# The last stage of an encoder layer: eight places for operand pieces, second halves loaded sooner, residual tiles in two sets

## The chip, the core and the metric

The kernel runs on one core of a Trainium2 chip. A core has a matrix engine (TensorE, PE in the rows), a vector engine (DVE), a scalar engine (ScalarE, ACT), GpSimd (POOL) and an engine that issues the transfers of this kernel (SyncE, SP; SPq is its queue). They run side by side, each takes its own instructions in a fixed order, and they wait for one another by semaphores. The metric is the time on the device in microseconds. TensorE's granted clock is given as a share of its full rate: 1.00 is the higher of its two levels, 2.4 GHz, and the lower one is 1.2 GHz.

## What is computed

One encoder layer on 9 blocks of 256 tokens (2048 of the prompt, 256 of the sample) with a model width of 1024. Cut to the part in which the change lies, with `o` the output of the gated linear attention (GLA), `y` that of the state-space branch (SSD) and `p` the embedding of each layer:

```python
def _layer(h, p, ...):
    u = _rmsnorm(h, norm_g)
    proj = u @ w_in                      # ... GLA gives o, SSD gives y
    o = _rmsnorm(o, gla_onorm_g).reshape(bt, L, GLA_VAL)
    o = o * jax.nn.silu(z_gla.astype(f32))
    y = y.reshape(bt, L, SSD_WIDTH) * jax.nn.silu(z_ssd.astype(f32))
    y = _rmsnorm(y, ssd_norm_g)
    mix = jnp.concatenate([o, y], axis=-1).astype(h.dtype)
    h = h + mix @ w_out
    e = _rmsnorm(p @ w_ple_proj, ple_norm_g)
    h = h + jax.nn.sigmoid(h @ w_ple_gate) * e
    return h
# trunk: _rmsnorm of the layer's output with final_norm_g
```

All is float32. Each product of two float32 matrices is made of three passes of rounded numbers: an operand is split into a rounded part (`_h`) and the rest (`_l`), and h·h, h·l and l·h are added up.

## The kernel before

Everything ahead of the last stage is the same in both kernels and isn't told here. The last stage, `output()` (L1232), works on blocks of 256 tokens and has three parts.

Part a, blocks 8 down to 0: `mix @ w_out` is split in two, and this is the GLA half. Four projections (`foa`, m = 0 to 3, 48 matmuls each) read the block's operand `fa{b}m`; the vector engine adds the residual tile `fx` (L1248) and SyncE stores the sum to `h1D`. The end of the stage before, the scan of the SSD branch (`s7b…`, `fz…zz`), still runs beside it and has its own few matmuls among the projections.

Part b, blocks 0 to 8: the SSD half, four projections `fob` from the operand `fb{b}m`, with the residual `fh` read back from `h1D` and the sum stored to `hD`.

Part c, the gate, blocks 0 to 8: class `Last` (L1135). Its `embed` makes `p @ w_ple_proj` (tiles `fl{b}e`), `load` (L1163) brings back the four tiles `fl{b}h` of h and splits each into a piece of the operand `fl{b}hh` (cast on the vector engine, L131, and the rest on GpSimd, L125), four projections `fpg` follow, `gate` (L1176) applies them (the product L1181 on the vector engine, the add L1182 and the sum of squares L1188 on GpSimd, squares on ScalarE), and `store` (L1226) multiplies the block with its norm (L1229) and writes the four tiles to `out` (L1230). In the loop (L1292 to L1310) the embedding of block b+1, the store of block b-1 and the load of block b+1 stand between the projections of block b.

An operand has four pieces, each with an h and an l tile of 128 x 2 x 256 (`new_u`, L151). They come from a pool with six places (`UBUFS`) for each of the two. A place comes free when the matmuls that read it are done, and a tile that is to take it waits for that. In parts a and b an operand (`mix_block`, L814) is made of two halves: each loads a raw tile (two places), scales it by the norm on the vector engine (L827; in part a by rows `fa{b}r` that SyncE loads, in part b by one made of `fb{b}r`), and splits it. The first half is issued with the operand, the second by `rest()`: in part a behind projection 2 of the block before (ahead of m = 3; for the last one ahead of m = 2), in part b ahead of m = 3.

Other tiles come from a second pool by tags: `dk` has 6 places and holds `fx` and `fh`, `mx` 7, `zo` 4, `eb` 2, `t4k` 2 and `y1` 10; `y1` holds the h tiles of the gate, four for each block. A scheduler walks through the program and fixes each engine's order; places that are handed out by the pools take part in it. So an edit of where a tile lies changes the order on all engines.

Of the kernel before, what the change touches and what calls it, by code (L numbers as in the profile page):

```python
# [9 lines left out]
F32R = mybir.dt.float32r  # L10
# [5 lines left out]
P = 128  # L16
T = 256
C = 128
NBP, NBS = 8, 1
NB = NBP + NBS  # L20
NT = NB * T
KT = 8
QMAX = 2
UK = 2
UBUFS = 6
# [8 lines left out]
def hybrid(ctx, tc, xT, pT, wsec, wsmall, wlast, wproj, wgate, bgate, norm_g, gla_g,  # L34
# [115 lines left out]

    def new_u(name):  # L151
        return [tuple(upool.tile([P, UK, T], F32R, name=f"{name}_{q}{n}", tag=f"u{q}", bufs=UBUFS)
                      for q in ("h", "l")) for n in range(KT // UK)]

    class Operand:

        def __init__(self, name, piece):
            self.parts, self.piece = new_u(name), piece
            for n in range(2):
                piece(n, *self.parts[n])  # L160
# [85 lines left out]
    with ExitStack() as mctx:  # L246
# [566 lines left out]

        def mix_block(b, half, r, name):  # L814

            raws = {}

            def piece(n, hi, lo):
                if n % 2 == 0:
                    r2 = upool.tile([P, 2, UK, T], F32, name=f"{name}_r{n}", tag="uraw", bufs=2)  # L820
                    sy.dma_start(r2, mixD[b][4 * half + n:4 * half + n + 2].rearrange("s p f t -> p s f t"))
                    raws[n], raws[n + 1] = r2[:, 0], r2[:, 1]
                raw = raws.pop(n)
                for k in range(UK):
                    kk = UK * n + k
                    g = g_gla[:, kk % 2:kk % 2 + 1] if half == 0 else g_ssd[:, kk:kk + 1]
                    ve.scalar_tensor_tensor(raw[:, k, :], raw[:, k, :], g, r(kk), ALU.mult, ALU.mult)  # L827
                split(raw, hi, lo, sc, po)
            return Operand(name, piece)

# [9 lines left out]
        def gla_mix(b, nm):  # L840
            r = [tmp("zo", [P, 2, T], f"{nm}r{j}") for j in range(2)]
            for j in range(2):
                rows(r[j], rD[b][2 * j:2 * j + 2])
            return mix_block(b, 0, lambda k: r[k // 4][:, k // 2 % 2, :], nm + "m")

# [23 lines left out]
        for i, s in enumerate(secs):  # L869
# [3 lines left out]
            for n, b in enumerate(s.order):  # L873
# [81 lines left out]
                u = u2  # L955
# [153 lines left out]
        def ssd_mix(b, nm):  # L1109
# [7 lines left out]
            def norm():  # L1117
                ps = bank("p2", [P, T], nm + "ps")
                total(ps, s, "hl", nm + "hl", ve, ve)
                rstd(ps, r, 1024.0, eps4)  # L1120
                return lambda: mix_block(b, 1, lambda k: r, nm + "m")

# [12 lines left out]
        class Last:  # L1135
# [27 lines left out]
            def load(self):  # L1163

                self.h = [tmp("y1", [P, 2, T], f"{self.nm}h{n}") for n in range(4)]
                self.uh = new_u(self.nm + "hh")
                for n in range(4):
# [64 lines left out]
        def output(nm, wo, u, first):  # L1232
# [3 lines left out]
            for b in range(NB - 1, -1, -1):  # L1236
                u2 = gla_mix(b - 1, f"{nm}a{b - 1}") if b else first_ssd()
                for m in range(4):
                    if m == (3 if b else 2):
                        u2.rest()  # L1240
                    x = tmp("dk", [P, 2, T], f"{nm}x{b}_{m}")
                    sy.dma_start(x, xT[b][:, 2 * m:2 * m + 2, :])
# [14 lines left out]
                if first:  # L1257
# [3 lines left out]
                    carry.append(lambda a=(s, bb, gate_z(z, f"{nm}z{bb}")): second(*a))  # L1261
            wp = [[tmp("xr" if q == 0 else "t4k", [P, 2, 512], f"{nm}wp{q}{j}", F32R) for j in range(2)] for q in range(2)]
            for b in range(NB):
# [4 lines left out]
                for m in range(4):  # L1268
                    if m == 3 and b + 1 < NB:
                        u2.rest()  # L1270
                    h = tmp("dk", [P, 2, T], f"{nm}h{b}_{m}")
                    sy.dma_start(h, h1D[b][:, 2 * m:2 * m + 2, :])
# [7 lines left out]
                    if b == NB - 1:  # L1280
# [3 lines left out]
                        wg.append(load_w(wlast[8 + m], f"{nm}g{m}"))  # L1284
                if b == NB // 2:
                    for j in range(2):
# [114 lines left out]
```

## Time and profile before

| | us |
|---|---|
| three runs | 2570.76, 2571.09, 2573.41 |
| median | 2571.09 |
| the profiled execution | 2570.19 |
| its span in the trace | 2568.5 |
| mean granted clock | 0.977 |

The profiled execution is 0.9 us below the median, and 1.7 us of it lie outside its span. In that span TensorE is busy for 2435.1 us (95%), the vector engine for 67%, ScalarE for 48% and GpSimd for 25%. The last stage runs from about 1749 us to the end: part a to 2007, part b to 2232, the gate from there on. In a row a duration of several like instructions in sequence is their sum ("x4"), and what stands in brackets at its end is how long the engine stood idle before it, and which instruction ended that. A granted clock below 1.00 means slower matmuls in a part of the stretch, and their cost comes on top of the idle time.

### The profile page before, as it was taken

The page shows a single profiled execution, that of the slowest core. Times are in us where ns is not written, and L with a number is a line of the kernel's source. Part 1 is how long each engine was busy: PE and PEld are TensorE (multiplying, and loading weights), DVE is VectorE, ACT ScalarE, POOL GpSimd, SP SyncE. Part 2 cuts the span into 40 slices and gives each one's busy share as a digit, 9 for nine tenths or more (in the row PEclk, how much of TensorE's full clock was granted, in tenths as well). Part 3 has the DMA queues.
Part 4 walks back from the last instruction along what each step waited for, and adds up shares of the span by engine and source line. Part 5 has one row for each costly group of instructions (what it writes and reads, how often), then busy time and mean ns, then how long its engine had stood idle before and what let it go on. Part 6 is the DMA issues. An engine that isn't in the chain of part 4 may idle for free.

```text
span 2568.5 us, 51535 instructions
## 1 busy us (share of the span) xinstructions
PE 2435.1 (95%) x19736; PEld 2373.7 (92%) x19736; DVE 1723.3 (67%) x4012; ACT 1225.5 (48%) x2468; POOL 638.5 (25%) x649
## 2 busy tenths in 40 slices
PE   7999999899999989999989999998999999998887
PEld 7999999799999979999989999998899999998886
DVE  8886799864579984468997456899633434544444
ACT  5565456644445654445565344565312323355545
POOL 3231000143200023320002330002444433354452
PEclk9999999899999999999999999999999999999988
DMA  6456466444655644465564446555765765412121
GB/s 235 161 175 196 154 181 206 154 139 146 217 169 166 194 143 161 146 205 170 168 215 138 137 154 214 168 164 176 230 196 186 239 184 159 133 38 75 38 75 60
DMA packets 295593, 415.05 MB, mean 162 GB/s; under 512 B 33020, under 2 KB 140328, under 8 KB 295336
## 3 DMA queue, kind: packets, MB, share of 16 engines
q1 hardware_dynamic: 295336, 411.66, 51.0%
q8 instruction: 157, 2.57, 0.4%
q14 instruction: 100, 0.82, 0.1%
HBM read 319.21 MB, written 92.35 MB: 160 GB/s over the span
## 4 chain that ended last, share of the span: by engine, by line
PE 58%; DVE 15%; DMA 10%; ACT 6%; issue 6%; POOL 4%; SPq 1%; DVEq 0%; POOLq 0%; ACTq 0%
PE pz L184 3%; PE pz L185 3%; PE pz L183 3%; PE pxb L183 2%; PE pxb L185 2%; PE pxb L184 2%; PE pxa L183 2%; PE fob L184 2%; PE pxa L184 2%; PE pxa L185 2%; PE fob L185 2%; PE fob L183 2%; PE pv L183 2%; PE pv L185 2%; PE pq L183 2%
## 5 line engine op out<-in xcount | busy, mean ns | idle before, releaser
L183 PE MATMUL pz<-u_h,wh_n 128*128 128x256 f32 x896 | 255.6, 285 | 0.0
L185 PE MATMUL pz<-u_h,wl_n 128*128 128x256 f32 x896 | 255.6, 285 | 0.0
L184 PE MATMUL pz<-u_l,wh_n 128*128 128x256 f32 x896 | 255.2, 285 | 0.0
L185 PEld LDWEIGHTS pz<-u_h,wl_n 128*128 128x128 f32 x896 | 171.0, 191 | 0.8 <-issue 0.7
L184 PEld LDWEIGHTS pz<-u_l,wh_n 128*128 128x128 f32 x896 | 171.0, 191 | 0.7 <-issue 0.7
L183 PEld LDWEIGHTS pz<-u_h,wh_n 128*128 128x128 f32 x896 | 171.0, 191 | 0.2
L183 PE MATMUL pxb<-u_h,wh_n 128*128 128x256 f32 x512 | 147.5, 288 | 0.0
L184 PE MATMUL pxa<-u_l,wh_n 128*128 128x256 f32 x512 | 147.2, 288 | 0.0
L183 PE MATMUL pxa<-u_h,wh_n 128*128 128x256 f32 x512 | 146.9, 287 | 0.0
L184 PE MATMUL pxb<-u_l,wh_n 128*128 128x256 f32 x512 | 146.3, 286 | 0.0
L185 PE MATMUL pxb<-u_h,wl_n 128*128 128x256 f32 x512 | 145.8, 285 | 0.0
L185 PE MATMUL pxa<-u_h,wl_n 128*128 128x256 f32 x512 | 145.4, 284 | 0.0
L183 PE MATMUL pq<-u_h,wh_n 128*128 128x256 f32 x384 | 113.3, 295 | 0.8 <-DVE z_0zz L805 0.5
L183 PE MATMUL pv<-wh_n,u_h 128*128 128x256 f32 x384 | 110.9, 289 | 0.7 <-DVE s4b1dm L508 0.2
L185 PE MATMUL pv<-wh_n,u_l 128*128 128x256 f32 x384 | 111.5, 290 | 0.0
L185 PE MATMUL pq<-u_h,wl_n 128*128 128x256 f32 x384 | 111.4, 290 | 0.0
L184 PE MATMUL pq<-u_l,wh_n 128*128 128x256 f32 x384 | 111.3, 290 | 0.0
L184 PE MATMUL pv<-wl_n,u_h 128*128 128x256 f32 x384 | 108.7, 283 | 0.0
L183 PEld LDWEIGHTS pxa<-u_h,wh_n 128*128 128x128 f32 x512 | 98.0, 191 | 1.6 <-issue 1.4
L183 PEld LDWEIGHTS pxb<-u_h,wh_n 128*128 128x128 f32 x512 | 97.9, 191 | 0.7 <-issue 0.7
L184 PEld LDWEIGHTS pxa<-u_l,wh_n 128*128 128x128 f32 x512 | 98.0, 191 | 0.5 <-issue 0.2
L184 PEld LDWEIGHTS pxb<-u_l,wh_n 128*128 128x128 f32 x512 | 97.8, 191 | 0.5 <-issue 0.5
(5981 smaller groups left out, 9539.6 us busy)
## 6 DMA issues: line engine op xcount, KB each, us to landing
u_h<-uD SPq DMA_DIRECT2D x224, 256.0 KB
u_l<-uD SPq DMA_DIRECT2D x224, 256.0 KB
wr_n<-wsec SPq DMA_DIRECT2D x48, 512.0 KB
fx<-xT SPq DMA_DIRECT2D x36, 256.0 KB
h1D<-fx SPq DMA_DIRECT2D x36, 256.0 KB
fh<-h1D SPq DMA_DIRECT2D x36, 256.0 KB
hD<-fh SPq DMA_DIRECT2D x36, 256.0 KB
wr_oa<-wlast SPq DMA_DIRECT2D x8, 512.0 KB
```

What stands on the lines that cost most here:

```text
L183: te.matmul(outs, lhsT=lh, rhs=rh, start=start and k == ks[0], stop=False, skip_group_check=True)
L184: te.matmul(outs, lhsT=lh, rhs=rl, start=False, stop=False, skip_group_check=True)
L185: te.matmul(outs, lhsT=ll, rhs=rh, start=False, stop=stop and k == ks[-1], skip_group_check=True)
```

## The change

Operands get eight places for pieces, by placing the second half of every other operand somewhere else. The second half of the GLA operands of even blocks below 7 and of the SSD operands of odd blocks below 7 lies in `t4k` (one tile for the h and the l of a piece); that of SSD block 7 and of the gate's even blocks lies in `eb` (piece 2) and `y1` (piece 3: two of the ten places). `rest()` is called ahead of m = 1 in part a and of m = 2 in part b. The residual tiles of odd m lie in `mx` (in part a for blocks below 7, in part b for all). The tiles of `wproj`, which use `t4k` too, are made and loaded behind block 6 of part b, no longer ahead of it and behind block 4.

```diff
-    def new_u(name):
-        return [tuple(upool.tile([P, UK, T], F32R, name=f"{name}_{q}{n}", tag=f"u{q}", bufs=UBUFS)
-                      for q in ("h", "l")) for n in range(KT // UK)]
+    def new_u(name, tags=()):
+        parts = []
+        for n in range(KT // UK):
+            tag = tags[n - 2] if tags and n >= 2 else None
+            if tag == "t4k":
+                t = tmp(tag, [P, 2, UK, T], f"{name}_{n}", F32R)
+                parts.append((t[:, 0], t[:, 1]))
+            elif tag:
+                parts.append(tuple(tmp(tag, [P, UK, T], f"{name}_{q}{n}", F32R) for q in "hl"))
+            else:
+                parts.append(tuple(upool.tile([P, UK, T], F32R, name=f"{name}_{q}{n}", tag=f"u{q}", bufs=UBUFS)
+                                   for q in ("h", "l")))
+        return parts
...
+            tags = ("t4k", "t4k") if b < NB - 2 and b % 2 == 0 else ()
+            return mix_block(b, 0, lambda k: r[k // 4][:, k // 2 % 2, :], nm + "m", tags)
...
+                tags = () if b % 2 == 0 else ("t4k", "t4k") if b < NB - 2 else ("eb", "y1")
+                return lambda: mix_block(b, 1, lambda k: r, nm + "m", tags)
...
-                self.uh = new_u(self.nm + "hh")
+                self.uh = new_u(self.nm + "hh", () if self.b % 2 else ("eb", "y1"))
...
-                    if m == (3 if b else 2):
+                    if m == (1 if b else 2):
                         u2.rest()
-                    x = tmp("dk", [P, 2, T], f"{nm}x{b}_{m}")
+                    x = tmp("mx" if m % 2 and b < NB - 2 else "dk", [P, 2, T], f"{nm}x{b}_{m}")
...
-            wp = [[tmp("xr" if q == 0 else "t4k", [P, 2, 512], f"{nm}wp{q}{j}", F32R) for j in range(2)] for q in range(2)]
...
-                    if m == 3 and b + 1 < NB:
+                    if m == 2 and b + 1 < NB:
                         u2.rest()
-                    h = tmp("dk", [P, 2, T], f"{nm}h{b}_{m}")
+                    h = tmp("mx" if m % 2 else "dk", [P, 2, T], f"{nm}h{b}_{m}")
...
-                if b == NB // 2:
+                if b == NB - 3:
+                    wp = [[tmp("xr" if q == 0 else "t4k", [P, 2, 512], f"{nm}wp{q}{j}", F32R) for j in range(2)]
+                          for q in range(2)]
```

Where this moves instructions. First GpSimd in part b, around the operand of block 1 (`fb1m_l` is the split, L1113 and L1115, then L1125 and L1127, make the sums of squares `fb2r` and `fb3r` for the norms of blocks 2 and 3). Before:

```order
L125 TENSOR_TENSOR fb1m_l_26154<-fb1m_r_26159,fb1m_h_26153 128x512
L1113 TENSOR_TENSOR fb2r_26285<-fb2r_26285,fb2r_26286 128x512
L1115 TENSOR_TENSOR fb2r_26285<-fb2r_26285 128x256
L1113 TENSOR_TENSOR fb3r_26539<-fb3r_26539,fb3r_26540 128x512
L125 TENSOR_TENSOR fb1m_l_26156<-fb1m_r_26222,fb1m_h_26155 128x512
L1115 TENSOR_TENSOR fb3r_26539<-fb3r_26539 128x256
L125 TENSOR_TENSOR fb1m_l_26158<-fb1m_r_26222,fb1m_h_26157 128x512
```

and after, where the second half of the operand (now one tile, `fb1m`) stands ahead of both sums:

```order
L125 TENSOR_TENSOR fb1m_l_26142<-fb1m_r_26145,fb1m_h_26141 128x512
L125 TENSOR_TENSOR fb1m_26143<-fb1m_r_26155,fb1m_26143 128x512
L125 TENSOR_TENSOR fb1m_26144<-fb1m_r_26155,fb1m_26144 128x512
L1125 TENSOR_TENSOR fb2r_26271<-fb2r_26271,fb2r_26272 128x512
L1127 TENSOR_TENSOR fb2r_26271<-fb2r_26271 128x256
L1125 TENSOR_TENSOR fb3r_26525<-fb3r_26525,fb3r_26526 128x512
L1127 TENSOR_TENSOR fb3r_26525<-fb3r_26525 128x256
```

Both sums moved behind the last two splits of block 1. Next SyncE in the gate, at the store of block 3, with what each transfer waits for. Before:

```order
L1168 DMA fl5h_30123<-hD_191 128x512 [waits DMAHW6_49,DMAHW2_49]
L1140 DMA fl5pr<-pT 128x512 [waits DMAHW7_49]
L1168 DMA fl5h_30124<-hD_191 128x512 [waits DMAHW3_49]
L1230 DMA out<-fl3h_29379 128x512 [waits DVE_49]
L1230 DMA out<-fl3h_29380 128x512 [waits DVE_49,Activation_49]
L1230 DMA out<-fl3h_29381 128x512 [waits DVE_49,Activation_49]
L1230 DMA out<-fl3h_29382 128x512 [waits DMAHW4_49,DVE_49,Activation_49]
L1168 DMA fl5h_30125<-hD_191 128x512 [waits DMAHW5_49,DMAHW1_49]
L1168 DMA fl5h_30126<-hD_191 128x512 [waits DMAHW6_49,DMAHW2_49]
```

After:

```order
L1243 DMA out<-fl3h_29365 128x512 [waits DMAHW7_49,DVE_49]
L1243 DMA out<-fl3h_29366 128x512 [waits DVE_49,Activation_49]
L1243 DMA out<-fl3h_29367 128x512 [waits DVE_49,Activation_49]
L1243 DMA out<-fl3h_29368 128x512 [waits DMAHW2_49,DVE_49,Activation_49]
L1181 DMA fl5h_30109<-hD_191 128x512 [waits DMAHW7_49,DMAHW3_49]
L1181 DMA fl5h_30110<-hD_191 128x512 [waits DMAHW4_49,DMAHW0_49]
L1181 DMA fl5h_30111<-hD_191 128x512 [waits DMAHW5_49,DMAHW1_49]
L1153 DMA fl6pr<-pT 128x512 [waits DMAHW6_49]
L1181 DMA fl5h_30112<-hD_191 128x512 [waits DMAHW2_49]
L1181 DMA fl6h_30481<-hD_192 128x512 [waits PE_49,Pool_49]
L1181 DMA fl6h_30482<-hD_192 128x512 [waits PE_49]
```

The first two loads of block 5 moved from ahead of the stores to behind them, and the first two of block 6 now wait for TensorE. Last, GpSimd in the gate, in the turn of block 4 (`fl3h` at the end is the last add of block 3, `fl3g0acc` its sum of squares). Before:

```order
L125 TENSOR_TENSOR fl4hh_l_29760<-fl4h_29753,fl4hh_h_29759 128x512 [waits DMAHW4_49,DVE_49]
L1188 TENSOR_TENSOR fl3g0acc<-fl3g0acc,fl3g2sq 128x512 [waits Activation_49]
L125 TENSOR_TENSOR fl4hh_l_29762<-fl4h_29754,fl4hh_h_29761 128x512 [waits DMAHW5_49,DVE_49]
L125 TENSOR_TENSOR fl5hh_l_30128<-fl5h_30123,fl5hh_h_30127 128x512 [waits DMAHW6_49,DVE_49]
L125 TENSOR_TENSOR fl5hh_l_30130<-fl5h_30124,fl5hh_h_30129 128x512 [waits DMAHW0_49,DVE_49]
L1182 TENSOR_TENSOR fl3h_29382<-fl3h_29382,fl3e_29474 128x512 [waits DVE_49]
L1188 TENSOR_TENSOR fl3g0acc<-fl3g0acc,fl3g3sq 128x512 [waits Activation_49]
```

After:

```order
L125 TENSOR_TENSOR fl4hh_l_29746<-fl4h_29739,fl4hh_h_29745 128x512 [waits DMAHW4_49,DVE_49,PE_49]
L1201 TENSOR_TENSOR fl3g0acc<-fl3g0acc,fl3g2sq 128x512 [waits Activation_49]
L125 TENSOR_TENSOR fl4hh_l_29748<-fl4h_29740,fl4hh_h_29747 128x512 [waits DMAHW5_49,DMAHW3_49,DVE_49]
L1195 TENSOR_TENSOR fl3h_29368<-fl3h_29368,fl3e_29460 128x512 [waits DMAHW0_49,DVE_49]
L1201 TENSOR_TENSOR fl3g0acc<-fl3g0acc,fl3g3sq 128x512 [waits Activation_49]
```

The two splits of block 5's first half are gone from between; in the turn of block 5 four splits of block 5 stand ahead of the add of block 4, and two of block 6 behind it.

## Rows read from the trace of the kernel before

**Rows 1.** The page's first line.
```profile
span 2568.5 us, 51535 instructions
```

**Rows 2.** TensorE's waits in the last stage: waiter, awaited, us in total, times, longest.
```profile
PE fob L184 <- POOL fb1m_l L125: 5.5, 1, 5.5
...
PE fob L184 <- POOL fb6m_l L125: 1.9, 2, 1.7
```

**Rows 3.** Stretches: us, busy time of PE, PEld, DVE, ACT, POOL, granted clock, DMA share, GB/s.
```profile
1855.00:1887.00 32.00, 26.74 (x204) 26.54 (x203) 11.90 (x19) 4.55 (x8) 14.99 (x16) 0.89 0.59 184
1887.00:2007.00 120.00, 120.00 (x1006) 120.00 (x1005) 48.01 (x78) 26.06 (x38) 60.86 (x62) 1.00 0.63 197
2031.00:2061.00 30.00, 24.53 (x194) 24.33 (x193) 8.49 (x17) 6.38 (x9) 11.34 (x11) 0.94 0.66 203
2061.00:2180.00 119.00, 117.06 (x975) 116.65 (x974) 45.31 (x76) 33.33 (x43) 37.43 (x30) 1.00 0.58 173
2261.00:2290.00 29.00, 29.00 (x244) 28.90 (x243) 14.29 (x21) 17.93 (x33) 14.00 (x11) 1.00 0.03 10
2290.00:2521.00 231.00, 197.73 (x1469) 191.82 (x1468) 107.23 (x158) 118.12 (x217) 114.15 (x84) 0.91 0.20 62
```

**Rows 4.** Timeline of PE at the gate's block 5: start, us, operation, count, idle before.
```profile
2404.74 0.28 PE L183 MATMUL fpg<-fl5hh_h,wh_fg 128*128 128x256 f32 x1
...
2412.15 0.58 PE L183 MATMUL fpg<-fl5hh_h,wh_fg 128*128 128x256 f32 x1 [4.37 <-DVE fl5hh_h L131]
...
2414.08 0.41 PE L183 MATMUL fpg<-fl5hh_h,wh_fg 128*128 128x256 f32 x1
2414.29 0.41 PE L184 MATMUL fpg<-fl5hh_l,wh_fg 128*128 128x256 f32 x1
```

**Rows 5.** Timeline in part a, block 5: what ends TensorE's wait there.
```profile
1853.90 1.30 POOL L125 TENSOR_TENSOR fa5m_l<-fa5m_r,fa5m_h 128x512 fp32r<-128x512 f32 x1
...
1859.26 0.80 SPq L812 DMA_DIRECT2D fa4r<-rD  x2
...
1861.10 0.38 SPq L821 DMA_DIRECT2D fa4m_r<-mixD  x1
...
1867.24 1.67 DVE L827 SCALAR_TENSOR_TENSOR fa4m_r<-fa4m_r,g_gla,fa4r 128x256 f32<-128x256 f32 x4 [7.40 <-DMA fa4m_r<-mixD]
...
1869.90 1.01 PE L761 MATMUL s7b2lpf<-s7b2qd,s7b2lS 128*128 128x128 f32 x3 [5.26 <-DVE s7b2lo L773]
```

**Rows 6.** Timeline in part b, block 1: GpSimd, and TensorE's use of fb2hl.
```profile
2031.84 1.29 POOL L1113 TENSOR_TENSOR fb2r<-fb2r,fb2r 128x512 f32<-128x512 f32 x1 [2.25 <-DMA fb2r<-sqD]
...
2036.85 1.26 POOL L1113 TENSOR_TENSOR fb3r<-fb3r,fb3r 128x512 f32<-128x512 f32 x1 [2.91 <-DMA fb3r<-sqD]
2038.07 1.26 POOL L125 TENSOR_TENSOR fb1m_l<-fb1m_r,fb1m_h 128x512 fp32r<-128x512 f32 x1
...
2049.34 0.28 PE L198 MATMUL fb2ps<-fb2hl,one 128*128 128x256 f32 x1
```

**Rows 7.** Timeline in the gate, block 4: from the cast to the products.
```profile
2372.14 0.43 DVE L131 CAST fl4hh_h<-fl4h 128x512 fp32r<-128x512 f32 x1 [4.57 <-DMA fl4h<-hD]
...
2378.38 3.59 POOL L125 TENSOR_TENSOR fl5hh_l<-fl5h,fl5hh_h 128x512 fp32r<-128x512 f32 x2 [1.64 <-DVE fl5hh_h L131]
2378.89 0.68 DVE L1181 SCALAR_TENSOR_TENSOR fl3e<-fl3g3th,fl3e 128x512 f32<-128x512 f32 x1
...
2381.93 1.29 POOL L1182 TENSOR_TENSOR fl3h<-fl3h,fl3e 128x512 f32<-128x512 f32 x1
...
2388.71 2.50 DVE L1174 TENSOR_TENSOR fl4e<-fl4e,fl4er 128x512 f32<-128x512 f32 x4 [2.60 <-ACT fl4er L240]
```

**Rows 8.** Timeline in the gate: the stores of block 3, loads and cast of block 5.
```profile
2402.18 3.67 SPq L1230 DMA_DIRECT2D out<-fl3h  x4
...
2405.95 0.90 SPq L1168 DMA_DIRECT2D fl5h<-hD  x2
...
2411.66 0.43 DVE L131 CAST fl5hh_h<-fl5h 128x512 fp32r<-128x512 f32 x1 [5.98 <-DMA fl5h<-hD]
```

More of the change, by code (lines that the diff above doesn't have):

```diff
@@ L149, in load_w, with __init__ @@
         return halves
-    def new_u(name):
-        return [tuple(upool.tile([P, UK, T], F32R, name=f"{name}_{q}{n}", tag=f"u{q}", bufs=UBUFS)
-                      for q in ("h", "l")) for n in range(KT // UK)]
+    def new_u(name, tags=()):
[11 more added lines that the diff above has]
+        return parts
     class Operand:
-        def __init__(self, name, piece):
-            self.parts, self.piece = new_u(name), piece
+        def __init__(self, name, piece, tags=()):
+            self.parts, self.piece = new_u(name, tags), piece
             for n in range(2):
@@ L812, in rows, with mix_block @@
                 sy.dma_start(dst[:, h, :], bass.AP(src.tensor, src.offset + h * T, [[0, P], [1, T]]))
-        def mix_block(b, half, r, name):
+        def mix_block(b, half, r, name, tags=()):
             raws = {}
@@ L828, in piece @@
                 split(raw, hi, lo, sc, po)
-            return Operand(name, piece)
+            return Operand(name, piece, tags)
         def gla_rstd(bs, nm):
@@ L843, in gla_mix @@
                 rows(r[j], rD[b][2 * j:2 * j + 2])
-            return mix_block(b, 0, lambda k: r[k // 4][:, k // 2 % 2, :], nm + "m")
+            tags = ("t4k", "t4k") if b < NB - 2 and b % 2 == 0 else ()
+            return mix_block(b, 0, lambda k: r[k // 4][:, k // 2 % 2, :], nm + "m", tags)
         pairs, wo = {}, []
@@ L1120, in norm @@
                 rstd(ps, r, 1024.0, eps4)
-                return lambda: mix_block(b, 1, lambda k: r, nm + "m")
+                tags = () if b % 2 == 0 else ("t4k", "t4k") if b < NB - 2 else ("eb", "y1")
+                return lambda: mix_block(b, 1, lambda k: r, nm + "m", tags)
             return norm
```

## The prediction

> **What bounds the kernel now.** The page comes first: one profiled execution, span 2568.5 us [rows 1]. All that is changed lies in the last stage, from about 1749 us to the end, so I read only that stretch. The list of TensorE's waits there shows where the matmuls stop [rows 2], and the table by stretches shows what a stop costs in all, because the granted clock is below 1.00 in the same stretches [rows 3]. Three kinds of place come out.
>
> Part a (four projections per block from the GLA operand) runs at 24.0 us a block where nothing disturbs it: five blocks from 1887 to 2007 take 120 us with TensorE busy throughout [rows 3]. The block before them takes 32, so 8.0 too much: 5.3 idle [rows 5] and 2.7 at a granted clock of 0.89 [rows 3]. Part b (the same from the SSD operand) has five blocks from 2061 to 2180 in 119 us, 23.8 each, but 30.0 for block 1: 5.5 idle and a clock of 0.94 [rows 2, 3]. Part c, the gate, has one undisturbed block, 29.0 us at clock 1.00 from 2261 to 2290; the next six take 231 us, 38.5 each [rows 3]. That is 231 - 6 x 29.0 = 57 us over its own best pace: 231 - 197.7 = 33 idle, and 24 of slower matmuls at a mean clock of 0.91. The half-speed pace is seen in the trace: after the wait that ends at 2412.15 the matmuls start 0.21 us apart (2414.08, 2414.29) [rows 4].
>
> **Part a.** TensorE waits 5.26 us, until 1869.90, for the vector engine's s7b2lo, which stands on that engine behind the scaling of fa4m_r; that waited 7.40 us for its load, and ran from 1867.24 for 1.67 [rows 5]. The load was issued only at 1861.10, behind the row load fa4r (1859.26). Its raw place comes free when GpSimd has made the second half of fa5m_l, which began at 1853.90 and stood behind other work there and, on ScalarE, behind a place of u. In the changed kernel the fa6 operand keeps its second half in a t4k place, fa5 finds its u places free, and the two splits stand four places earlier each on GpSimd, so they lie before 1853.90; SyncE issues the load of fa4m_r ahead of the fa4r rows. Issued at about 1854, and with the same 6.1 us from issue to use (1861.10 to 1867.24), fa4m_r is there at about 1860. Then fa4r's second rows are last: if they still go out at 1859.26 and take 6.1 us too, the scaling starts at 1865.4, 1.8 earlier than at 1867.24, and 3.4 of the wait are left; if they go out with the other load, s7b2lo comes before TensorE asks for it (1869.9 - 5.3 = 1864.6). So 0 to 3.4 us of wait are left, and I take 1, as nearer to the load that moves, with no slow clock behind it: 7 of the 8.0 are gained. The ends are 3 (fa4r late and the loads of fx, which also move up, in the way) and 8. In the five blocks from 1887 on TensorE has no idle time, so the eight places and the earlier second halves gain nothing there.
>
> **Part b.** GpSimd had two sums of squares for later blocks ahead of its split of block 1's second half: fb2r at 2031.84 after a wait of 2.25 us for a load, fb3r at 2036.85 after 2.91, and only then fb1m_l at 2038.07 [rows 6]. In the changed order the four pieces of block 1 stand together ahead of both. Both sums serve blocks 2 and 3, and TensorE takes up the first (fb2ps) at 2049.34 [rows 6], or 2043.9 without the stop; the fb2r sum, moved behind splits of 4 x 1.26, is done by about 2037. So they have 7 us of cover; without it they would cost up to the 5.2 of their two waits. I take 6 of the 6.2 excess (30.0 - 23.8), from 3 to 6.2. Block 6 waits 1.9 for its splits [rows 2]; there the order after still has one sum between, so I take 1, from -1 to 2. The residual loads fh and fx, now in two sets of tiles, go out earlier and no engine waits for them before, so they are worth nothing; they can only crowd other loads, which is in the lower ends above. Loading wproj behind block 6 is nothing too: TensorE needs it first in block 8, one block (23.8) later.
>
> **Part c.** Here the places of u are not what is late. The cast of a block's second half (block 4: 2372.14) waited 4.57 us for the load of h, and not for TensorE [rows 7]. Behind it on the vector engine stands fl3e (2378.89), on GpSimd the two splits of block 5's first half (3.59 us at 2378.38), and behind those the last add of block 3 (2381.93) [rows 7]. The add leads through the square, the sum, the vector engine's four products (2388.71) and the two halves of the sum, the table loads of rstd and the four products of store to the four stores (2402.18, 3.67 us), and only behind these come the loads of the next half (2405.95) and its cast (2411.66) [rows 7, 8]. One turn is 2411.66 - 2372.14 = 39.5 us, against 29.0 of matmuls.
>
> What changes: uh's last piece of an even block (0, 2, 4, 6, 8) takes two of the ten y1 places, so no spare pair is left for the odd block's first half; all four loads of an odd block now stand behind the four stores. So in an even block's turn the two splits of 3.59 us are gone from GpSimd ahead of the add, and the split sum is no longer behind the four products (2.50 at 2388.71 [rows 7]). Part of this lands in ScalarE's queue, so I take 3.4 off: 36.1. In an odd block's turn the splits ahead of the add are four as before, the third and fourth now being its own, and the next block's two come behind the add; the same replay with the durations of before gives 35.2 against 37.5 (77.0 for the pair, from 231 / 3, less 39.5). But TensorE loses something. Before, it did 24 matmuls of block 5 from 2404.74 on and then stood still until 2412.15 [rows 4]; now it stops ahead of the first one, for some 7 to 8 us, and does them afterwards at the slow pace: 24 x 0.21 = 5.0. An odd block is then 24 x 0.21 + (244 - 24) x 0.12 = 31.4 of matmuls (244 is block 1's number, and 29.0 / 244 = 0.12 [rows 3]) plus waits, some 33, still inside the turn. The pair comes to 71.3, three pairs give 3 x (77.0 - 71.3) = 17. The ends are 0 and 26 (half again). Block 8 and what follows move with the rest, unchanged.
>
> In block 5's turn the two splits took 3.59 us together beside casts and products of the vector engine, where a single one of the same size took 1.26 at 2038.07 [rows 6, 7]. "SBUF — State Buffer" of the Trainium skill, section "Who interferes with whom", says that GpSimd and the vector engine share one read path, and that an instruction with two inputs there can hold the other up whole. By that rule an odd block's four splits, now beside four casts, would each take the longer time of that row, 1.8 us and not 1.26: an estimate of 2 us per odd block, and 17 would be 11. The trace doesn't show them in that place.
>
> **The sum.** Against the profiled execution of 2570.19 (span 2568.5 and 1.7 outside it): -7 - 6 - 1 - 17 = -31, so 2539; the median of the runs shown is 0.9 above the profiled one, so 2540. I take 2541, since block 1 of the gate and the last block bring small waits of their own that the replay doesn't hold.
>
> **Rivals.**
> 1. The gate gives nothing. The turn is a chain over five engines, and a shorter piece can be swallowed by the next queue: ScalarE carries out a fixed order with table loads in it, and the vector engine's casts stand in one row with the products. For it: the cast waits for the load and not for a place [rows 7]. Against: the 3.59 stands right on the chain [rows 7]. Then only a and b are left, 14: 2557.
> 2. The gate loses, and the whole becomes slower: TensorE's path takes over. If the chain to the next cast follows from the odd block's matmuls and not from the stores, an odd block costs its wait of 7.5 and then 31.4 plus the waits of 3 to 4 that rstd brings, some 42, while the even one stays at 40 because its first half now waits for places that TensorE frees at the end of the block before last. A pair of 82 to 87 loses 5 to 10, three of them 15 to 30; with only the lower ends of a and b (3 + 3 - 1) the end is 2581 to 2596. With those lower ends it decides from a pair of 78.7 on (3 x 1.7 = 5), and by 0.2% from 80.4. "Perfetto Trace Analysis" of the Trainium skill, section "Identifying Performance Opportunities", names a gap that repeats as a sign of too few places for the next tile; by that the two y1 places taken here would cost the gate more than the u places give. The row says load after store [rows 7, 8], which is a shortage of y1 places too, so this rival is not empty.
> 3. The stops of a and b only move: fa4r's rows or a crowded load end 3 us later and part b's sums come late for block 2. Then they give 6 and not 14, with the gate as forecast: 2548.
> 4. The change does not do what it says: the places were not late anywhere, all three terms fall away, 2571. Against it speaks that the stop in b is a matter of order alone.
>
> **How the numbers follow.** Forecast (gate 10 to 26, a and b nearly whole) 0.50; rival 3 0.13; rival 1 0.20; rival 2 0.11; rival 4 0.06. The likeliest is 2541. Its own ends are 14 + 26 = 40 off (2531) and 10 + 10 off (2551); both ends of the range take in rivals 1 and 3 and a little of a larger gain: 2527 to 2569, which leaves out rival 2, most of rival 4 and the least likely of the others. Faster by more than 0.2% (5 us, about what can be told from no change) is the forecast, 3 and 1, and a part of what lies between: 0.83; within it 0.07; slower 0.10.
>
> **What would show it.** In the profile after: no wait for s7b2lo at about 1865 and the block in 24 to 25; no wait for fb1m_l, fb2r and fb3r behind it; in the gate pairs of 71, waits of TensorE of 7 to 8 us at the start of the odd blocks alone, and the add of the even blocks within 7 us of their cast (9.8 before). It would be wrong if the pairs stay at 77 (rival 1) or grow (rival 2), if the odd blocks' fourth load, which comes behind the pr load, keeps fl4e waiting, or if new waits come up for the pieces that now lie in y1 and eb.

## The result, and the profile after

The changed kernel takes 2533.11 us (median of 4 runs, 2530.25 to 2534.37) against 2571.16 for the kernel before (4 runs, 2570.76 to 2573.41): a ratio of 0.9849, 95% interval 0.9832 to 0.9866. That is 38 us less where 30 were forecast, inside the range of 2527 to 2569.

The page's first line of the changed kernel, which answers [rows 1], shows 36.3 us less:

```profile
span 2532.2 us, 51521 instructions
```

TensorE's waits in its last stage (waiter, awaited, us in total, times, longest), to be read against [rows 2]:

```profile
PE fb0ps L209 <- DVE fb0hl L131: 6.3, 1, 6.3
...
PE fpg L194 <- DVE fl5hh_h L131: 4.0, 1, 4.0
...
PE fl8zpt L1210 <- DVE fl8g0acc L1201: 4.0, 1, 4.0
...
PE fl5eps L209 <- DVE fl5ehl L131: 3.6, 1, 3.6
```

fb1m_l and fb6m_l, the waits of [rows 2], are gone from the list, and so is s7b2lo of [rows 5]. At its head stands a wait that the kernel before did not have, for fb0hl, the norm of block 0 of part b. The others shown belong to odd blocks of the gate and to the last one.

The stretches, from block to block, answer [rows 3] (us, busy time of PE, PEld, DVE, ACT, POOL, granted clock, DMA share, GB/s). They are, in order, part a's block 5, its block 1, part b's block 1, five blocks of part b, the gate's undisturbed block 0, its blocks 2 to 7, and the first three projections of its block 8:

```profile
1856.10:1880.00 23.90, 23.90 (x203) 23.90 (x202) 10.48 (x19) 5.24 (x9) 14.82 (x15) 1.00 0.80 254
...
1951.50:1984.50 33.00, 26.67 (x204) 26.25 (x203) 12.35 (x20) 8.82 (x13) 17.54 (x19) 0.90 0.50 160
2032.00:2055.20 23.20, 23.20 (x197) 23.20 (x196) 10.44 (x18) 6.68 (x10) 11.82 (x10) 1.00 0.66 209
2055.20:2171.20 116.00, 116.00 (x973) 116.00 (x971) 47.68 (x74) 29.95 (x40) 38.35 (x31) 1.00 0.48 148
2223.00:2252.10 29.10, 29.05 (x244) 28.87 (x243) 14.82 (x25) 16.34 (x32) 15.62 (x11) 1.00 0.09 28
2281.20:2489.30 208.10, 182.94 (x1466) 180.80 (x1465) 114.34 (x157) 119.95 (x217) 114.65 (x86) 0.93 0.22 71
2489.30:2507.00 17.70, 17.70 (x151) 17.70 (x150) 10.18 (x15) 7.57 (x12) 6.70 (x5) 1.00 0.00 1
```

The last of these has no row among those of before; there the same 151 matmuls took 24.3 us, in part at the lower clock level:

```profile
2521.20:2545.50 24.30, 21.16 (x151) 20.56 (x150) 12.76 (x19) 10.35 (x17) 9.21 (x7) 0.86 0.18 55
```

The accounts by the first matmul of each block, before and after:

| | before | after | difference | forecast |
|---|---|---|---|---|
| ahead of the last stage | 1749.3 | 1747.4 | -1.9 | 0 |
| part a, to part b's start | 257.5 | 260.9 | +3.4 | -7 |
| part b | 225.0 | 214.65 | -10.35 | -7 |
| gate, blocks 2 to 7 | 230.8 | 208.1 | -22.7 | -17 |
| gate, three projections of block 8 | 24.3 | 17.65 | -6.65 | 0 |
| rest of the gate (blocks 0, 1, the end) | 81.6 | 83.5 | +1.9 | 0 |
| all | 2568.5 | 2532.2 | -36.3 | -31 |

The first line is no effect: the profiled executions of all kernels shown here reach the last stage between 1747.2 and 1752.7, with the same instructions ahead of it. The stretches themselves repeat well: from the first matmul of the last stage to the second block of part b the changed kernel takes 284.6 us, and the two kernels below that share its parts a and b take 284.5 and 284.3. So the total came out near the forecast, but part a went the other way and the gate gave more. These two were tested.

### The profile page after: what moved, and what is told of

Same layout as the page of the kernel before. It is cut to its first block, busy times and chain, and to the rows that moved or that the text cites. A ratio compares the mean times of both kernels' runs of the same rounds, so it can differ in the third digit from the quotient of the medians.

```text
span 2532.2 us, 51521 instructions
## 1 busy us (share of the span) xinstructions
PE 2414.2 (95%) x19736; PEld 2358.0 (93%) x19736; DVE 1737.0 (69%) x4012; ACT 1227.8 (48%) x2468; POOL 639.1 (25%) x649
```

## Experiments: which of the places made the gate faster

**The three parts apart.** First the gate alone: everything in parts a and b as before.

```diff
-            tags = ("t4k", "t4k") if b < NB - 2 and b % 2 == 0 else ()
+            tags = ()
-                tags = () if b % 2 == 0 else ("t4k", "t4k") if b < NB - 2 else ("eb", "y1")
+                tags = ()
```

(and `rest()`, `fx`, `fh` and `wp` as in the kernel before.)

> The changed kernel with parts a and b put back (places, rest(), residual tiles, wproj), so only the gate's even blocks keep two pieces in eb and y1. Theory A (the gate's gain comes from the loads and splits of an odd block's first half going behind the store, and is independent of a and b): the gate takes about 309 us as in the changed kernel, the waits for s7b2lo (5.3) and fb1m_l (5.5) are back, fb0ps does not wait; 2571 - 27 = 2544. Rival (a and b carry the gain of the gate too, since it starts earlier or with other clocks): gate 320 or more, 2555 and up.

Measured: 2543.91, ratio 0.9893 (0.9872 to 0.9914). Blocks 2 to 7 of the gate take 207.5, and both old stops are back, s7b2lo with 5.2 and fb1m_l with 6.0. Then parts a and b alone:

```diff
-                self.uh = new_u(self.nm + "hh", () if self.b % 2 else ("eb", "y1"))
+                self.uh = new_u(self.nm + "hh")
```

> The changed kernel with the gate's operand back in the six places; parts a and b as changed. Theory A: gate back to 335 to 337 us, blocks 2 to 7 at 231; part b gains its 10, part a loses 3, some 2 earlier at the start of the stage: 2571 - 9 = 2562. Rival: gate stays at 320 or below, 2548 or less.

Measured: 2562.71, ratio 0.9963 (0.9948 to 0.9978); blocks 2 to 7 take 228.7, the wait for fb0hl is there with 6.4. So 28 us belong to the gate and 9 to parts a and b, together 37 of 38: the parts add up.

**Places, or the pair of `y1`?** The gate's edit does two things: an operand's pieces get more places, and two of the ten `y1` tiles are no longer free for the next block's h. With the last piece in `dk` the first remains and the second goes:

```diff
-                self.uh = new_u(self.nm + "hh", () if self.b % 2 else ("eb", "y1"))
+                self.uh = new_u(self.nm + "hh", () if self.b % 2 else ("eb", "dk"))
```

> The changed kernel with the gate's last piece in dk and not in y1: still eight places for pieces, but the spare pair of y1 is left for the odd blocks' first half, whose loads stand ahead of the stores again. Theory A: the turn of 77 for a pair is back, gate 330 to 337, 2533 + 23 = 2556 (2552 to 2562). Rival B (the eight places are what the gate wins by): gate 309 or less, 2533 or less.

Measured: 2556.51, ratio 0.9938 (0.9917 to 0.9959). A pair of blocks (3 and 4):

```profile
2323.70:2398.90 75.20, 65.45 (x490) 63.58 (x489) 41.18 (x52) 39.45 (x72) 37.00 (x28) 0.91 0.20 62
```

The next pair takes 75.7. With parts a and b alone the two pairs took 76.5 and 76.9, and in the changed kernel they take 69.1 and 68.8. Blocks 2 to 7 take 222.0, so more places alone give 6.7 (from the 228.7 above), but 4.3 of that lie in block 7 and only 1.3 and 1.2 in the two pairs. The counterpart is the kernel before with two `y1` tiles held through the whole gate and not one place more:

```diff
+            held = [tmp("y1", [P, 2, T], f"{nm}hold{n}") for n in range(2)]
+            for t in held:
+                ve.memset(t[:, 0, 0:2], 0.0)
...
+            for n, t in enumerate(held):
+                spare = tmp("q1", [P, 2], f"{nm}spare{n}")
+                ve.tensor_copy(spare, t[:, 0, 0:2])
```

> The kernel before with one addition: two y1 tiles are set and held through the gate, so the operand has its six places but no block has a spare pair for the next one's first half; all four loads of every block stand behind the stores. Theory A: every turn is like the changed kernel's (33 to 36), TensorE stops once in each block; blocks 2 to 7 take 200 to 216, 2571 - 22 = 2549. Rival B (places): the loads come later and nothing is won, the gate takes 337 to 360, 2571 to 2594.

Measured: 2556.74, ratio 0.9932 (0.9908 to 0.9956): 15 us faster than before with two tiles taken away. (The profiled execution shows 11.2 of it: the gate is 15.2 shorter there and part b 3.5 longer.) Blocks 2 to 7:

```profile
2297.90:2513.20 215.30, 189.26 (x1464) 187.24 (x1465) 110.61 (x156) 120.15 (x216) 111.31 (x84) 0.92 0.21 67
```

That is 15.5 less than the 230.8 of before. It falls short of the expected 22, and block 1 gets 3.4 longer. The 15.5 here and the 6.7 of the places come near the 22.7 of the change, but they don't divide it: this kernel takes the pair from every block, the change only from the odd ones. What is shown is that most of the gate's gain comes without one place more, from the pair that is no longer spare, and that the gate is another 7.2 shorter with the places added and the pair spare for the even blocks. Where that acts is seen in the turn of block 4 of the kernel with the pair held (cast, add of block 3, products of its store, cast of block 5):

```profile
2370.01 0.43 DVE L131 CAST fl4hh_h<-fl4h 128x512 fp32r<-128x512 f32 x1 [4.72 <-DMA fl4h<-hD]
```
```profile
2379.74 1.28 POOL L1182 TENSOR_TENSOR fl3h<-fl3h,fl3e 128x512 f32<-128x512 f32 x1 [0.63 <-DVE fl3e L1181]
```
```profile
2398.84 2.50 DVE L1229 TENSOR_TENSOR fl3h<-fl3h,fl3fr 128x512 f32<-128x512 f32 x4 [5.49 <-ACT fl3fr L240]
...
2405.18 0.43 DVE L131 CAST fl5hh_h<-fl5h 128x512 fp32r<-128x512 f32 x1 [3.24 <-DMA fl5h<-hD]
```

From cast to add it is 9.7, as before (9.8 [rows 7]), since here all four splits of block 4 itself stand ahead of the add; from products to cast it is 6.3 and was 10.2 (2401.46, shown below, to 2411.66 [rows 8]). So holding the pair shortens the end of the turn, by 3.9. The beginning is 7.1 in the changed kernel, 2.7 shorter, and neither experiment has that. With the places alone, in the turn of block 5 (cast, add of block 4), it is 9.8:

```profile
2399.63 0.43 DVE L131 CAST fl5hh_h<-fl5h 128x512 fp32r<-128x512 f32 x1 [5.12 <-DMA fl5h<-hD]
```
```profile
2409.45 1.29 POOL L1195 TENSOR_TENSOR fl4h<-fl4h,fl4e 128x512 f32<-128x512 f32 x1 [0.63 <-DVE fl4e L1194]
```

The 2.7 come only where a block's own first half is loaded early and the next block's is not, as in the even blocks of the change. Block 8's 6.65 also come with both only: it takes 24.2 and 24.6 in these two kernels.

## Experiments: where part a's gain went

The stop of [rows 5] is gone (block 5 takes 23.90), and four blocks later TensorE waits 6.33 us and runs at a clock of 0.90. The timeline of the changed kernel there (start, us, engine, what it did, idle before it and its releaser):

```profile
1964.53 0.93 SPq L1124 DMA_DIRECT2D fb0r<-sqD  x1
...
1971.52 1.26 POOL L1125 TENSOR_TENSOR fb0r<-fb0r,fb0r 128x512 f32<-128x512 f32 x1 [7.91 <-DMA fb0r<-sqD]
...
1974.85 1.33 DVE L131 CAST fb0hl<-fb0r 128x256 fp32r<-128x256 f32 x1 [9.88 <-POOL fb0r L1127]
...
1976.33 0.55 PE L209 MATMUL fb0ps<-fb0hl,one 128*128 128x256 f32 x1 [6.33 <-DVE fb0hl L131]
```

The load of fb0r goes out at 1964.53 and is used 7.0 us later, in a stretch in which the DMA engines are full:

```profile
1965.00:1972.00 7.00, 5.00 (x42) 4.79 (x40) 0.00 (x0) 0.00 (x0) 0.48 (x1) 1.00 1.00 337
```

Two experiments moved the ends of this chain. One put block 0's norm one projection later:

```diff
-                    elif b == 1 and m == 2:
+                    elif b == 1 and m == 3:
```

> The changed kernel with the norm of SSD block 0 (fb0ps) one projection later in GLA block 1. Theory A (TensorE stops 6.3 us there because the two loads of fb0r land late, behind 512 KB of raw operand, a weight and six stores that now go out together; nothing else is late): one projection is 5.9 us, so the wait falls to 0.5 or less, the slow clock behind it goes too, and nothing comes up in its place: 2533 - 8 = 2525. Rival (the operand of SSD block 0 is the next thing late, since its scaling waits for that norm): the stop moves to block 0 of part a or b, 2531 to 2536.

Measured: 2535.87, ratio 0.9861 (0.9844 to 0.9877); the stop is now in part b's block 0, at the scan's last steps. The other started block 0's sums earlier:

```diff
-                    if b == 1 and m == 0:
+                    if b == 2 and m == 2:
```

> The changed kernel with the loads of fb0r and its sum issued two projections sooner (GLA block 2), its norm where it was. Theory A (late loads): no wait for fb0hl, 2525. Rival (the four zo places are what is short: fb0r holds two of them, so fa0r comes later): a wait of some us for fa0m or s7b5lo or s7b6lo in block 1 or 2 takes the place of the 6.3, 2530 to 2538.

Measured: 2538.49, ratio 0.9868 (0.9852 to 0.9885); TensorE waits for s7b6lo. Then all of part a's edits undone:

```diff
-            tags = ("t4k", "t4k") if b < NB - 2 and b % 2 == 0 else ()
+            tags = ()
-                    if m == (1 if b else 2):
+                    if m == (3 if b else 2):
-                    x = tmp("mx" if m % 2 and b < NB - 2 else "dk", [P, 2, T], f"{nm}x{b}_{m}")
+                    x = tmp("dk", [P, 2, T], f"{nm}x{b}_{m}")
```

> The changed kernel with part a as before (six places, second half ahead of the last projection, residual tiles in dk). Theory A (part a gains 8 at block 5 and gives 9 back at block 1 and 2 at block 6): the wait for s7b2lo (5.3) is back and that for fb0hl gone, 2533 - 3 = 2530. Rival (part a's earlier end is worth its 8 and the stop at fb0 has to do with part b's places): 2538 to 2541.

Measured: 2534.94, ratio 0.9858 (0.9842 to 0.9875), not the 2530 expected: s7b2lo is back, fb0hl is gone, but a new wait for s7b8lo takes its place. By their times none of the three can be told from the changed kernel (0.9832 to 0.9866); what they show lies in the profiles. TensorE's longest wait from block 5 of part a to the end of part b, in the order of these three (norm later, sums earlier, part a undone with two rows):

```profile
PE fb1ps L209 <- DVE s7b8lo L784: 4.5, 1, 4.5
```
```profile
PE s7b6lpf L772 <- DVE s7b6lo L784: 9.7, 1, 9.7
```
```profile
PE s7b2lpf L772 <- DVE s7b2lo L784: 5.3, 1, 5.3
...
PE fb1ps L209 <- DVE s7b8lo L784: 2.3, 1, 2.3
```

From the first matmul of the last stage to the second block of part b these kernels take 286.0, 286.7 and 285.1; the changed kernel takes 284.6 and the one before 281.5. So moving one end only moved the stop, as the rivals of the first two had it. The scan that runs beside part a has to be through by then, and TensorE waits for it once or twice, wherever. What makes the scan late was asked next.

**Not the early second halves.** `rest()` as in the kernel before, the places as in the changed one:

```diff
-                    if m == (1 if b else 2):
+                    if m == (3 if b else 2):
...
-                    if m == 2 and b + 1 < NB:
+                    if m == 3 and b + 1 < NB:
```

> The changed kernel with rest() where it was before in parts a and b, so only places and tiles are changed. Theory A (places and order cure the stops at s7b2lo and fb1m_l; the earlier rest() is worth nothing): neither stop is back, 2533 within 3. Rival (the earlier loads are what cures them): both stops are back, part a and b lose 12 to 15, 2545 to 2548.

Measured: 2535.95, ratio 0.9865 (0.9848 to 0.9881); no old stop comes back, fb0hl stays with 6.5. The earlier calls are worth nothing that can be told here.

**Not the residual tiles in `mx`,** which other work uses as well:

```diff
-                    x = tmp("mx" if m % 2 and b < NB - 2 else "dk", [P, 2, T], f"{nm}x{b}_{m}")
+                    x = tmp("dk", [P, 2, T], f"{nm}x{b}_{m}")
```

> The changed kernel with the residual tiles of part a in dk alone, as before. Theory C (in the changed kernel the steps of the scan that runs beside part a come 26.3 us apart in blocks 3 to 5, slower than TensorE's 23.8, since the loads of fa2r, fa1r and fa0r stand on SyncE behind the loads of fx and z, which share mx now and wait there for stores; the vector engine then waits 7.5, 9.6 and 12.3 us for them, and the stop at fb0ps is what has added up): the steps are 23.9 apart again, the stop at fb0ps falls from 6.3 to under 2, 2533 - 8 = 2525. Rival (the residual tiles don't matter, the rows wait for their zo places): steps 26 apart, stop of 6, 2533 within 3.

Measured: 2542.2, ratio 0.989 (0.9875 to 0.9905), 9 us slower by the medians than the changed kernel where 8 faster were expected. The stop grows:

```profile
PE fb0ps L209 <- DVE fb0hl L131: 11.6, 1, 11.6
```

So the theory that they stood in the scan's way falls, and the second set of tiles has a value.

**The row loads behind SyncE's queue.** VectorE's waits between 1885 and 1980 (scaling of part a's raw tiles), in the changed kernel:

```profile
DVE fa1m_r L838 <- DMA fa1r<-rD: 14.2, 3, 9.6
DVE fa0m_r L838 <- DMA fa0r<-rD: 14.1, 2, 12.3
DVE fa2m_r L838 <- DMA fa2r<-rD: 11.5, 3, 7.5
```

and in the kernel before, the longest of its kind, ahead of it the wait on which VectorE spent its idle time there, for TensorE's projections:

```profile
DVE fx L1248 <- PE foa L185: 42.5, 15, 5.1
...
DVE fa2m_r L827 <- DMA fa2r<-rD: 2.4, 1, 2.4
```

VectorE stands still for 39.8 us in all for rows that are not there, where it stood for 42.5 before because it was ahead of TensorE (that wait is 8.9 now). The scan's own steps stand behind the rows: they come 26.6 apart (1898.1, 1924.6, 1951.2) where they came 23.5 apart before (1899.5, 1922.7, 1946.6) beside blocks of 23.9. On SyncE the row loads (128 KB each, four for a block) stand behind the loads of fx (256 KB), which wait there until the store of the tile that had the place before is done. SyncE's waits for these stores in the same stretch, in the changed kernel and before:

```profile
SPq L1255 <- DMA h1D<-fx: 20.3, 7, 4.7
```
```profile
SPq L1242 <- DMA h1D<-fx: 25.4, 15, 2.7
```

So these waits are not new, and the first rows of block 1 go out about when they did (1917.6, and 1915.9 before). But TensorE and VectorE are 7 us further there than before, and the rows did not move up with them. The timeline also shows why they don't: in the changed kernel the adds into fx stand on VectorE behind the scaling with the rows (1904.0 to 1906.7), their stores free the tiles, the next loads of fx wait for these, and the next rows stand behind those. That this ring sets the 26.6 is a reading of the timeline; the next experiment cuts it at one place.

To take the rows from behind these loads, the row loads alone go out from ScalarE's queue (`rows`, one word):

```diff
-                sy.dma_start(dst[:, h, :], bass.AP(src.tensor, src.offset + h * T, [[0, P], [1, T]]))
+                sc.dma_start(dst[:, h, :], bass.AP(src.tensor, src.offset + h * T, [[0, P], [1, T]]))
```

> The changed kernel with the row loads of the GLA operands (fa..r) issued from ScalarE's queue, so that they pass SyncE's. Theory C: rows no longer stand behind the loads of fx and z, the waits of the vector engine for them are 3 or less, no stop at fb0ps, 2525; 2528 if the loads hold up ScalarE's own work a little. Rival (zo places): the rows come at the same time as before, the stop stays, 2533 or more, since ScalarE's casts now wait behind them.

Measured: 2529.62, ratio 0.9838 (0.9824 to 0.9851), so the time alone can't be told from the changed kernel's. VectorE's longest wait for rows in the same stretch:

```profile
DVE fa1m_r L838 <- DMA fa1r<-rD: 6.3, 1, 6.3
```

That is more than the 3 expected, but half of the 12.3. The first two rows of block 1 now go out at 1905.8 and 1909.5 instead of 1917.6 and 1919.4. The scan's steps are 24 apart again (1894.4, 1918.4, 1942.6), and from block 5 of part a to the start of part b's second block TensorE runs through; this kernel, and below it the changed one in the same stretch:

```profile
1856.50:2024.20 167.70, 167.27 (x1403) 167.10 (x1402) 70.93 (x112) 39.77 (x56) 85.23 (x84) 1.00 0.70 221
```
```profile
1856.10:2032.00 175.90, 169.57 (x1402) 169.15 (x1401) 71.08 (x113) 39.50 (x57) 84.30 (x83) 0.98 0.67 213
```

With blocks 8 to 6 that is 273.8 against 284.6 for part a and part b's first block, 10.8 less (274.4 in the last kernel below, which has the same parts a and b). Part a alone takes 250.1, 7.4 less than in the kernel before: the gain that was forecast. The fx loads still wait on SyncE (30.1 us between 1885 and 1980); only the rows no longer stand behind them. That is the cause, shown by taking it away: the change removed one late load of part a, the rows of later blocks came late in its place, and both fed the same chain. It also speaks against the rival that the rows wait for their `zo` places, at least for the first two rows of a block; the other two go out right behind the scan's step in all these kernels. Which of its edits brought the rows there is not settled. With all of part a's edits undone VectorE's waits for rows are 2.3 at most; `rest()` alone or `mx` alone did not take them away. That leaves the places in `t4k`, by themselves or with one of the others, and they were not tried alone.

Both together, fx in `dk` alone and the rows from ScalarE:

> Both: residual tiles of part a in dk alone, and the row loads on ScalarE's queue. Theory C: each alone takes the stop away, so both together win no more than one: 2525 within 3. Rival (zo places): stop stays, 2533 or more.

Measured: 2528.43, ratio 0.9833 (0.9817 to 0.985). A wait of 2.7 for fb0hl is left; the stretch takes 276.8, 3.0 longer than with two sets of tiles. So the premise that each edit alone takes the stop away was wrong, and with the rows out of the queue the second set is worth about 3 us in the profile, too little to tell by the times.

## Experiment: VectorE beside GpSimd in the gate

The four products of VectorE ahead of the gate (L1187) took 5.79 us in block 5 of the changed kernel, with splits of GpSimd beside them:

```profile
2396.43 5.79 DVE L1187 TENSOR_TENSOR fl5e<-fl5e,fl5er 128x512 f32<-128x512 f32 x4
```
```profile
2396.19 3.19 POOL L125 TENSOR_TENSOR fl6hh_l<-fl6h,fl6hh_h 128x512 fp32r<-128x512 f32 x2
2399.34 1.73 POOL L1201 TENSOR_TENSOR fl4g0acc<-fl4g0acc,fl4g3sq 128x512 f32<-128x512 f32 x1
```

In block 4 of the kernel before, the same four took 2.50 [rows 7]. On top of the rows from ScalarE, the first two splits of every block went to VectorE:

```diff
-                    split(self.h[n], *self.uh[n], ve, po)
+                    split(self.h[n], *self.uh[n], ve, ve if n < 2 else po)
```

> The kernel with the row loads on ScalarE's queue, and the low halves of the gate's first two pieces of every block split on VectorE instead of GpSimd. Contention theory: the four products of VectorE that took 5.8 us beside GpSimd's splits in the odd turns, and 2.50 with GpSimd idle, fall to about 2.5 to 3.5, the chain of the last block's finish shortens by as much, the odd turns go from about 35 to 33.5, and the time is 1.5 times three less, about 2525. Rival (the odd turn is TensorE's own path, and VectorE's queue only gets longer): the odd turns stay at 35 or grow, and the time is 2530 or more.

Measured: 2526.14, ratio 0.9825 (0.9811 to 0.9839). The products, now with GpSimd idle until 2394.12:

```profile
2391.65 2.49 DVE L1187 TENSOR_TENSOR fl5e<-fl5e,fl5er 128x512 f32<-128x512 f32 x4 [1.86 <-ACT fl5er L251]
```

and without the edit, on the kernel with the rows on ScalarE:

```profile
2388.14 5.80 DVE L1187 TENSOR_TENSOR fl5e<-fl5e,fl5er 128x512 f32<-128x512 f32 x4
```

The time is near that of the contention theory, but not for its reason. Blocks 3 to 6, two pairs, without and with the edit:

```profile
2308.70:2445.80 137.10, 121.82 (x977) 120.69 (x977) 75.98 (x104) 79.62 (x145) 76.47 (x57) 0.92 0.22 70
```
```profile
2308.60:2445.80 137.20, 124.02 (x977) 122.09 (x977) 66.88 (x113) 78.64 (x144) 64.33 (x48) 0.95 0.21 70
```

The turn is the same: 137.1 and 137.2. An odd block gets 3 shorter (35 to 32), and the even one behind it 3 longer (33.4 to 36.4), because its end still waits for the same stores and loads. So the slowing of the products beside GpSimd is shown (5.80 and 2.49). What it costs is not: the two splits that VectorE took over run 1.67 each and stand ahead of the products, which end at 2394.1 with the edit and at 2393.9 without it. The two spans are 2524.8 and 2524.1; the 3.5 us between the medians have no place in the profiles, and the intervals overlap.

This kernel and the other two with the rows on ScalarE are the fastest that were run. Their intervals still overlap that of the changed kernel (up to 0.9839, 0.9850 and 0.9851, against 0.9832 and more), so that they beat it is shown for part a in the profile and not for the whole time.

## Why the prediction was right, and where it was not

**Part a: the step on the stop held, the term did not.** The wait for s7b2lo vanished as worked out (block 5 from 31.8 to 23.9, a gain of 7.9 for 7; blocks 8 to 6 took 2.7 longer, so that 5.1 were won when it ended). But "gain nothing" for the five blocks behind it was taken as "lose nothing". The scan beside them had kept TensorE's pace, with VectorE often waiting for TensorE. With 26.6 a step, where a block takes 23.9, it fell back by 2.7 in each block until TensorE had to wait for fb0hl, in block 1 (33.1, and 24.1 before). The fall was named as rival 3 (a stop that only moves), by fa4r's rows in block 5; it was the rows of blocks 2 to 0. Its price was 8 for parts a and b together, and part a alone came out 10 worse than forecast. What failed is that SyncE's queue was read at block 5 only, and the edit moves it in every block.

**Part b: right, a little small.** -10.35 for -7. Block 1 gave 7.2 (6 forecast) and block 6 2.5 (1 forecast), and no sum came late for block 2. The pace of an undisturbed block had been taken as 23.8 from a stretch that held block 6's own wait; without that wait such a block takes 23.3 in the kernel before and 23.2 in the changed one.

**The gate: the step on the add held, and the larger part of the gain came where none was forecast.** As forecast the odd blocks wait at their start and the even ones do not, and the add of block 3 comes 7.1 us behind block 4's cast (within 7 was forecast, 9.8 before [rows 7]). The timeline of the changed kernel answers [rows 4, 7, 8], from cast to cast:

```profile
2351.80 0.43 DVE L131 CAST fl4hh_h<-fl4h 128x512 fp32r<-128x512 f32 x1 [4.09 <-DMA fl4h<-hD]
...
2358.90 1.29 POOL L1195 TENSOR_TENSOR fl3h<-fl3h,fl3e 128x512 f32<-128x512 f32 x1 [2.24 <-DVE fl3e L1194]
...
2378.71 2.50 DVE L1242 TENSOR_TENSOR fl3h<-fl3h,fl3fr 128x512 f32<-128x512 f32 x4 [4.56 <-ACT fl3fr L251]
2379.43 2.17 SPq L1243 DMA_DIRECT2D out<-fl3h  x4
2381.70 1.64 SPq L1181 DMA_DIRECT2D fl5h<-hD  x3
...
2385.09 0.43 DVE L131 CAST fl5hh_h<-fl5h 128x512 fp32r<-128x512 f32 x1 [3.28 <-DMA fl5h<-hD]
2385.66 0.98 PE L194 MATMUL fpg<-fl5hh_h,wh_fg 128*128 128x256 f32 x3 [4.05 <-DVE fl5hh_h L131]
...
2390.27 0.58 PE L209 MATMUL fl5eps<-fl5ehl,one 128*128 128x256 f32 x1 [3.63 <-DVE fl5ehl L131]
```

The even turn takes 33.3 (36.1 forecast, 39.5 before), the odd one 35.6 (35.2 forecast). Of the 6.2 that the even turn gained, 2.7 lie between cast and add, for the 3.4 forecast. The replay kept the old durations for the rest, and there lies the error: from the products of store to the next load it is 2.99 (2378.71 to 2381.70) where it was 4.5, since the four products took 3.61 before, beside an add of GpSimd, and now 2.50 alone:

```profile
2401.46 3.61 DVE L1229 TENSOR_TENSOR fl3h<-fl3h,fl3fr 128x512 f32<-128x512 f32 x4 [4.04 <-ACT fl3fr L240]
```
```profile
2402.03 1.29 POOL L1188 TENSOR_TENSOR fl4g0acc<-fl4g0acc,fl4g1sq 128x512 f32<-128x512 f32 x1 [1.99 <-ACT fl4g1sq L1186]
```

(both of the kernel before). And the load is used 3.4 us after its issue instead of 5.7 [rows 8]. These are 1.5 and 2.3, with the 2.7 about the 6.2, so 3.8 of the turn's gain are no part of the forecast's mechanism. Holding the pair brings this end of the turn (6.3, and 6.4 here); why the load can be used sooner behind its issue stays open.

The wait ahead of an odd block's first matmul was to be 7 to 8; it is 4.05, with 3.63 more ahead of the embedding's norm. Together that is what was forecast, split in two.

**"Block 8 and what follows unchanged" was wrong.** Block 8 has an even block's places, and there the wait of 2.2 and the slow clock behind it went as in the other even blocks: -6.65. The end lost 2.2, of which 1.4 are a longer wait for the final sum (4.0, 2.6 before).

**"Worth nothing" for the residual tiles was wrong, for the early `rest()` right.** Without the second set part a stops for 11.6 instead of 6.3, and the time is 9 us longer; with the rows out of SyncE's queue it is worth about 3. The prediction's "nothing" for the earlier second halves was for part a's five blocks; they turned out to be worth nothing in parts a and b as a whole.

**The rivals.** The one that ended slower (the pair of `y1` taken away makes TensorE wait for h) had its sign reversed: held pairs alone made the kernel 15 us faster. "Perfetto Trace Analysis" of the Trainium skill, section "Identifying Performance Opportunities", says that a repeating gap can mean too few places; that holds for the smaller part of this gap: more places alone gave 6.7, two places less gave 15.5.

**The rule on the shared path.** "SBUF — State Buffer" of the Trainium skill, section "Who interferes with whom", would by the prediction's estimate have made the odd blocks' splits 1.8 us each and the gate's gain 11. The four splits of block 5 took 1.28, 1.44, 1.41 and 1.34. The rule agrees with the trace on the other engine: VectorE's products of two inputs took 5.79 and 3.61 beside GpSimd and 2.50 without it. What that costs the gate no run here shows.

**The sum** came close by luck, because two errors met: part a 10.4 worse than its term, the gate 10.5 better and part b 3.4.

## What to carry to other kernels

A spare buffer is not free: here two tiles less made the gate 15 us shorter. An early load brings its follow-up work onto the queues of other engines, ahead of work that the loop's chain may wait for (2.7 us in a turn here); so ask what stands there on each engine before more places are given out, and try a place less. Where a stop disappears, the main loop runs ahead of a chain beside it: ask for every later block, and not for the one with the stop alone, whether what that chain waits for moves up too. Here its rows did not, and the stop came back four blocks on; when they did, it was gone. Loads that an engine's queue of work waits for don't belong behind a load that itself waits for its tile.

## What the runs showed of the hardware

The same four products of two inputs (128x512) on VectorE took 2.49 to 2.50 us with GpSimd idle, 3.61 beside one add of GpSimd and 5.79 beside three of its instructions, while GpSimd's own took up to 1.73 in place of 1.29. That VectorE takes up to 2.3 times as long and GpSimd about a third longer was not expected.

A transfer behind others on SyncE's queue waits for theirs: in the changed kernel the first rows of block 1 went out behind a load of fx, at 1917.6, and VectorE waited up to 12.3 us for a load of rows. Issued from ScalarE, they went out at 1905.8, and the longest wait was 6.3.
